# Rows of x turned and scaled in one product with a diagonal, and the modulation's weights behind x: the start of a hybrid decoder layer

## The chip, the cores and the metric

The kernel runs on one core of a Trainium2 chip, as one launch. The metric is device time in microseconds (us) of that core. Engines are named as the profile names them: PE is TensorE (matrix products; PEld is its weight load), DVE VectorE, ACT ScalarE, POOL GpSimd, SP SyncE. SPq and ACTq are the sequencers of SP and ACT as issuers of transfers.

## The reference, cut

One layer of a decoder trunk, batch 1, 512 tokens, width 2048, all float32. What matters here is its first lines:

```python
mod = silu(c) @ w_ada + b_ada                  # 1 x 6144
shift, scale, gate = split(mod, 3)
u = rms_norm(x, norm_w) * (1.0 + scale) + shift  # 512 x 2048
proj = u @ w_in                                # 512 x 23552
# ... three token mixers (attention, retention, dilated windows), each with its
# gate and projection, a gated sum m of the three, and
x = x + gate * (m @ w_out);  out = rms_norm(x, final_norm_w)
```

where `rms_norm(x, w) = x * rsqrt(mean(x*x) + 1e-6) * w`.

## The kernel before, in words

**Products.** A float32 product is done as three products of split operands. `h` is the value cast to PE's faster float32 form (`fp32r`), `l` the value minus `h`; then `uh*wh + ul*wh + uh*wl` go into one accumulator. So each weight tile needs a cast on ACT (`wh`) and a subtraction on DVE (`wl`, called the low part here), and each column block of u a `uh` on ACT and a `ul` on DVE. PE then runs three products of 512 columns for each block.

**The start.** u must stand with its 2048 channels on the partitions: 16 blocks k of 128 channels by 512 tokens, `xT[:, k, :]` before the modulation. x comes as 4 token tiles of 128x2048 (`xt[0..3]`, 1 MB each). For each tile ACT squares it and sums (`ss`), takes the root (`rstd`), DVE takes the reciprocal and multiplies the tile by it (`x_scale`); PE turns its 16 blocks with an identity (`x_tr`, 64 turns in all), and ACT copies each k from PSUM to `xT`. The small vectors (c, norm_w, b_ada and two more) come as 82 rows of `smalls` in five transfers and are turned on PE in one step to `cols`.

**The modulation.** The scale half of `mod` is worked out on DVE, not on PE: `mod_sum(m, part)` takes one 1 MB piece `wa` of w_ada and adds its rows, each times one entry of silu(c), into an accumulator `acc`; `mod_cols(m)` sums `acc` over the partitions with products against a column of ones (`pj<-ones,acc`), and two short DVE steps make `s1 = norm_w * (1 + scale)` of the group. `MODS` lists the groups: (half, first column, width). A group of 128 columns is one piece and 16 DVE steps of 128 columns, and gives `s1` for one k; a group of 256 is two pieces and 16 steps of 256 columns, for two k. Then `scaled(k)` makes `uh[k]` and `ul[k]` of `xT` and `s1`.

**Two passes over k.** The loop over `steps` has phase 0 (`uh`, `ul` without the shift; 16 steps of 21 products, 7 column blocks of w_in, on 7 accumulators) and phase 1 (with the shift, 16 such steps). Between the two, `spill` copies the seven accumulators to `raw` (two buffers) on ACT and DVE in turn, each copy followed by a transfer `graw` to memory on ACT's queue, and two more column blocks are done alone with four weight tiles of 128x1024 (`mids`, called the middle stage here; each tile needs its `wh` on ACT and its `wl` on DVE). During phase 0 DVE also does the sums of later groups (`mod_step`); the shift half (`sh`) is needed at the first step of phase 1. After that come the bulk of the projections, the mixers and the output, some 2370 us that this change leaves alone.

**What sets the order.** Each engine runs its instructions in a fixed order. At the places here a scheduler sets it when the kernel is built, by its own costs and by what is ready; `tc.issue_after(i)` holds a group of instructions behind instruction i, and `pin` (active where `pinned[0]` is true) keeps an engine's instructions in the order in which the code is written. Every recorded operation bears line 86 (`pin`) or its neighbour, so groups are told apart by the names of their tiles. SP issues all loads of x, `wa` and `wr` in one queue, in the order of the code; `wa` has 4 buffers, `wb` 3.

Of the kernel before, what the change touches and what calls it, by code (L numbers as in the profile page):

```python
# [65 lines left out]
def hybrid_kernel(ctx, tc, x, c, w_in, w_pa, w_pb, w_pc, w_out, w_ada, b_ada, norm_w, lam,  # L66
# [36 lines left out]
    def at():  # L103
        return psum.tile([P, 512], F32, tag="at", name="at", bufs=6)
# [120 lines left out]
    sync.dma_start(out=smalls[0:16, :], in_=c.rearrange("o (j p) -> (o j) p", p=P))  # L225
    sync.dma_start(out=smalls[16:32, :], in_=norm_w.rearrange("o (j p) -> (o j) p", p=P))
    sync.dma_start(out=smalls[32:80, :], in_=b_ada.rearrange("o (j p) -> (o j) p", p=P))
    sync.dma_start(out=smalls[80:81, :], in_=da_w)
    sync.dma_start(out=smalls[81:82, :], in_=ret_w)
# [11 lines left out]
    def mod_load():  # L241
        if not to_load:
            return
        i = len(parts) - len(to_load)
        m, part = to_load.pop(0)
        half, c0, cw = MODS[m]
        nk = 2048 // cw
        if i < 6 or (i - 6) % 7 >= 3:
            wa = sp.tile([P, nk, cw], F32, tag="wa", name="wa", bufs=4)
        else:  # L250
            wa = wb[0].tile([P, nk, cw], F32, tag="wb", name="wb", bufs=3)
        sync.dma_start(out=wa, in_=w_ada[0, part * nk * P:(part + 1) * nk * P, half * D + c0:half * D + c0 + cw]
                          .rearrange("(j p) c -> p j c", p=P))
        wa_tiles[m, part] = wa
# [101 lines left out]
    tps = [at() for _ in range(6)]  # L356
    for i in range(3):
        act.activation(out=xTf[:, i * D:(i + 1) * D], in_=xt[i], func=AF.Square, accum_out=ss[:, i:i + 1])
        if i == 0:
            act.activation(out=sgc, in_=c_col, func=AF.Sigmoid)  # L360
            dve.tensor_scalar(out=eps0, in0=sgc[:, 0:1], scalar1=0.0, scalar2=EPS, op0=ALU.mult, op1=ALU.add)
            dve.tensor_mul(sc, c_col, sgc)
            dve.tensor_scalar_mul(daw, cols[:, 80:81], 1.0 - LAM_INIT)
        x_scale(i)
        if i == 1:
            m, part = to_sum.pop(0)
            mod_sum(m, part)
        for k in range(6):
            x_tr(tps[k], i, k)
    for q in range(2):  # L370
        act.activation(out=xTf[:, 3 * D + q * 1024:3 * D + (q + 1) * 1024], in_=xt[3][:, q * 1024:(q + 1) * 1024],
                       func=AF.Square, accum_out=ss[:, 3 + q:4 + q])
    dve.tensor_add(ss[:, 3:4], ss[:, 3:4], ss[:, 4:5])
    x_scale(3)
    mod_cols(0)
# [6 lines left out]
    for k in range(KC):  # L382
        tp = tps[k] if k < 6 else at()
        for i in range(3 if k < 6 else 0, NT):
            x_tr(tp, i, k)
        act.copy(xT[:, k, :], tp)
        if k == 0:
            scaled(0)
            split_first(0)
            m, part = to_sum.pop(0)  # L390
            mod_sum(m, part)
            mod_cols(m)
        if k == 4:
            split_first(1)
# [14 lines left out]
    for i, (phase, k) in enumerate(steps):  # L409
# [1362 lines left out]
```

## Time and profile before

| what | value |
|---|---|
| median of 3 runs | 2574.26 us (2572.38 to 2576.52) |
| the profiled execution: its time, its span | 2571.79 us, 2570.0 us |
| mean granted clock of PE in it | 0.995 of full speed |
| PE busy | 2516.9 us, 98% |
| DVE busy | 1907.0 us, 74% |
| ACT busy | 1134.4 us, 44% |
| first main product of PE (`uh` by `wh`) | at 30.83 us |

The profile is one execution; its times run from the start of its span, and the 1.79 us between span and time lie around it. A busy share is an average over stages with different limits: what bounds one stage is read from that stage alone.

### The profile page before, as it was taken

The page shows a single profiled execution, that of the slowest core. Times are in us where ns is not written, and L with a number is a line of the kernel's source. Part 1 is how long each engine was busy: PE and PEld are TensorE (multiplying, and loading weights), DVE is VectorE, ACT ScalarE, POOL GpSimd, SP SyncE. Part 2 cuts the span into 40 slices and gives each one's busy share as a digit, 9 for nine tenths or more (in the row PEclk, how much of TensorE's full clock was granted, in tenths as well). Part 3 has the DMA queues.
Part 4 walks back from the last instruction along what each step waited for, and adds up shares of the span by engine and source line. Part 5 has one row for each costly group of instructions (what it writes and reads, how often), then busy time and mean ns, then how long its engine had stood idle before and what let it go on. Part 6 is the DMA issues. An engine that isn't in the chain of part 4 may idle for free. (4 is left out here: it accounts for less than half of the span.)

```text
span 2570.0 us, 36726 instructions
## 1 busy us (share of the span) xinstructions
PE 2516.9 (98%) x14539; PEld 2224.0 (87%) x14539; DVE 1907.0 (74%) x2716; ACT 1134.4 (44%) x1476; POOL 179.9 (7%) x293
## 2 busy tenths in 40 slices
PE   7999999999999999999999999999999999999998
PEld 6787777999999999999887888888888888778888
DVE  7885888778887788877886777347887657786554
ACT  5233433443444333333336666346666436652223
POOL 0000000000000000000000001200000220003100
PEclk9999999999999999999999999999999999999999
DMA  9886765666666666666556555654333673439533
GB/s 346 294 293 233 253 213 213 218 209 212 234 233 228 220 209 231 236 223 231 208 183 198 153 160 146 198 162 118 109 113 107 191 222 98 118 113 297 190 133 113
DMA packets 363953, 504.83 MB, mean 196 GB/s; under 512 B 18850, under 2 KB 237748, under 8 KB 363396
## 3 DMA queue, kind: packets, MB, share of 16 engines
q1 hardware_dynamic: 329732, 401.89, 47.8%
q0 software_dynamic: 27136, 92.13, 10.4%
q10 hardware_dynamic: 6912, 8.46, 0.9%
q8 instruction: 114, 1.87, 0.3%
q14 instruction: 59, 0.48, 0.1%
HBM read 450.37 MB, written 52.04 MB: 195 GB/s over the span
## 5 line engine op out<-in xcount | busy, mean ns | idle before, releaser
L86 ACT CAST xh<-xr 128x2048 fp32r<-128x2048 f32 x196 | 374.3, 1910 | 589.7 <-PE at L86 478.8
L86 DVE TENSOR_TENSOR xl<-xr,xh 128x2048 fp32r<-128x2048 f32 x196 | 448.9, 2290 | 184.9 <-ACT xh L86 183.5
L86 DVE TENSOR_TENSOR wl<-wr,wh 128x1024 fp32r<-128x1024 f32 (+2 forms) x275 | 275.4, 1018 | 186.2 <-ACT wh L86 181.4
L86 PE MATMUL pj<-uh,wl 128*128 128x512 f32 x944 | 368.6, 390 | 3.6 <-DVE wl L86 3.6
L86 PE MATMUL pj<-uh,wh 128*128 128x512 f32 x944 | 371.8, 394 | 0.0
L86 ACT CAST wh<-wr 128x1024 fp32r<-128x1024 f32 (+2 forms) x275 | 239.3, 889 | 294.8 <-PE at L86 137.9
L86 PE MATMUL pj<-ul,wh 128*128 128x512 f32 x944 | 368.5, 390 | 0.0
L86 DVE TENSOR_TENSOR xr<-xr 128x512 f32<-128x512 f32 x448 | 309.3, 690 | 13.8 <-DMA xr<-in_w_in_dram 2.3
L86 PE MATMUL at<-fh,xl 128*128 128x256 f32 x864 | 244.9, 283 | 0.7 <-DVE xl L86 0.7
L86 PE MATMUL at<-fh,xh 128*128 128x256 f32 x864 | 244.5, 283 | 0.0
L86 PE MATMUL at<-fl,xh 128*128 128x256 f32 x864 | 244.5, 283 | 0.0
L86 PEld LDWEIGHTS pj<-uh,wl 128*128 128x128 f32 x944 | 177.7, 188 | 41.7 <-DVE wl L86 4.0
L86 PEld LDWEIGHTS pj<-ul,wh 128*128 128x128 f32 x944 | 177.9, 188 | 35.4
L86 PEld LDWEIGHTS pj<-uh,wh 128*128 128x128 f32 x944 | 177.7, 188 | 35.3
L86 PEld LDWEIGHTS at<-fh,xl 128*128 128x128 f32 x864 | 165.8, 192 | 0.9 <-DVE xl L86 0.9
L86 PEld LDWEIGHTS at<-fh,xh 128*128 128x128 f32 x864 | 165.8, 192 | 0.0
L86 PEld LDWEIGHTS at<-fl,xh 128*128 128x128 f32 x864 | 165.8, 192 | 0.0
L86 PE MATMUL at<-uh,xh 128*128 128x256 f32 x576 | 163.0, 283 | 0.0
L86 PE MATMUL at<-ul,xh 128*128 128x256 f32 x576 | 163.0, 283 | 0.0
L86 PE MATMUL at<-uh,xl 128*128 128x256 f32 x576 | 163.0, 283 | 0.0
L86 PE MATMUL at<-yh,wh 128*128 128x512 f32 x288 | 113.1, 393 | 2.2 <-ACT wh L86 2.2
L86 PE MATMUL at<-yh,wl 128*128 128x512 f32 x288 | 112.8, 391 | 0.1
(387 smaller groups left out, 5595.5 us busy)
## 6 DMA issues: line engine op xcount, KB each, us to landing
xr<-in_w_in_dram SPq DMA_DIRECT2D x224, 512.0 KB, 4.5
xr<-in_w_in_dram SPq DMA_DIRECT2D x84, 1024.0 KB, 4.9
wr<-in_w_in_dram SPq DMA_DIRECT2D x116, 512.0 KB, 4.2
wa<-in_w_ada_dram SPq DMA_DIRECT2D x20, 1024.0 KB, 8.3
wr<-in_w_out_dram SPq DMA_DIRECT2D x32, 512.0 KB, 3.9
wr<-in_w_in_dram SPq DMA_DIRECT2D x32, 448.0 KB, 7.6
wb<-in_w_ada_dram SPq DMA_DIRECT2D x12, 1024.0 KB
bw<-in_w_in_dram SPq DMA_DIRECT2D x24, 384.0 KB, 5.5
```

Of the source, the lines that this page charges most:

```text
L86: return lambda *a, **k: pin(f(*a, **k))
```

## The change

It touches the start up to the first step of phase 0, and one condition in the loop.

1. The five transfers of `smalls` are issued by ACT, ahead of everything else there; SP's queue begins with x, in eight halves of 512 KB, all of them ahead of the first `wa`. Before, two tiles of x, the first `wa`, and then the other two.
2. The tiles of x are not scaled. For each tile ACT squares two halves (into the end of `xT`, which is free then), DVE adds the two sums, ACT takes the root, and DVE the reciprocal; then DVE makes `diag[i] = identity * rstd`, 128x128, and PE multiplies each block of x with it: `x_block.T @ diag` is turned and scaled at once. It is a true float32 product in place of a turn; there are 64, as there were turns.
3. Tiles 0 and 1 go first, as a pair: their 24 products for the first 12 blocks k, and DVE copies these to `xT` in six steps of two blocks by 256 tokens (a seventh a little later); tiles 2 and 3 follow. The other nine copies are ACT's.
4. `MODS` begins with four groups of 128 columns (two before).
5. The whole start is pinned to the order of the code, to the low part of the first weight tile; what of the sums comes after is held behind that low part.

```diff
-    sync.dma_start(out=smalls[0:16, :], in_=c.rearrange("o (j p) -> (o j) p", p=P))
...
+    pinned[0] = True
+    act.dma_start(out=smalls[0:16, :], in_=c.rearrange("o (j p) -> (o j) p", p=P))
...
-    for i in range(2):
-        sync.dma_start(out=xt[i], in_=x[0, i * P:(i + 1) * P, :])
-    MODS = [(1, 0, 128), (1, 128, 128)] + [(1, c0, 256) for c0 in range(256, D, 256)] \
+    for i in range(NT):
+        for q in range(2):
+            qs = slice(q * 1024, (q + 1) * 1024)
+            sync.dma_start(out=xt[i][:, qs], in_=x[0, i * P:(i + 1) * P, qs])
+    MODS = [(1, c0, 128) for c0 in range(0, 512, 128)] + [(1, c0, 256) for c0 in range(512, D, 256)] \
...
-    sync.dma_start(out=xt[2], in_=x[0, 2 * P:3 * P, :])
-    for q in range(2):
-        sync.dma_start(out=xt[3][:, q * 1024:(q + 1) * 1024], in_=x[0, 3 * P:4 * P, q * 1024:(q + 1) * 1024])
...
+    act.activation(out=sgc, in_=c_col, func=AF.Sigmoid)
+    dve.tensor_scalar(out=eps0, in0=sgc[:, 0:1], scalar1=0.0, scalar2=EPS, op0=ALU.mult, op1=ALU.add)
+    act.activation(out=warm, in_=eps0, func=AF.Sqrt)
+    dve.tensor_mul(sc, c_col, sgc)
...
+    def x_squares(i):
+        for q in range(2):
+            act.activation(out=junk, in_=xt[i][:, q * 1024:(q + 1) * 1024], func=AF.Square,
+                           accum_out=ss[:, 2 * i + q:2 * i + q + 1])
+        dve.tensor_add(ss[:, 2 * i:2 * i + 1], ss[:, 2 * i:2 * i + 1], ss[:, 2 * i + 1:2 * i + 2])
+        act.activation(out=rstd[:, i:i + 1], in_=ss[:, 2 * i:2 * i + 1], func=AF.Sqrt, scale=1.0 / D, bias=eps)
+    def x_norm(i):
         dve.reciprocal(rstd[:, i:i + 1], rstd[:, i:i + 1])
-        for q in range(2):
-            qs = slice(q * 1024, (q + 1) * 1024)
-            dve.tensor_scalar_mul(xt[i][:, qs], xt[i][:, qs], rstd[:, i:i + 1])
-    def x_tr(tp, i, k):
-        pe.transpose(tp[:, i * P:(i + 1) * P], xt[i][:, k * P:(k + 1) * P], ident)
...
+        dve.tensor_scalar_mul(diag[i], ident, rstd[:, i:i + 1])
+    def x_turn(tps, i, ns):
...
+                pe.matmul(tps[n][:, o * P:(o + 1) * P], lhsT=xt[i][:, (2 * n + k) * P:(2 * n + k + 1) * P],
+                          rhs=diag[i], start=True, stop=True)
+    def x_put(tps, pair, ns, copy):
+        for n in ns:
+            copy(xT[:, 2 * n:2 * n + 2, pair * 256:pair * 256 + 256], tps.pop(n).rearrange("p (k t) -> p k t", k=2))
+    x_squares(0)
+    x_norm(0)
+    x_squares(1)
+    x_norm(1)
+    x_turn(tps, 0, range(6))
+    x_turn(tps, 1, range(6))
+    x_put(tps, 0, range(6), dve.tensor_copy)
+    for i in range(2):
+        x_turn(tps, i, (6,))
+    x_squares(2)
+    x_norm(2)
+    x_put(tps, 0, (6,), dve.tensor_copy)
+    x_turn(tps, 2, range(6))
+    x_squares(3)
+    x_norm(3)
...
+    mod_sum(m, part)
+    for n in range(6):
+        x_turn(tps, 3, (n,))
+    x_put(tps, 1, range(5), act.copy)
+    x_turn(tps, 2, (6, 7))
+    x_turn(tps, 3, (6, 7))
+    mod_cols(0)
...
+    halves[0] = act.copy(firsts[0][1], firsts[0][0]).ins
+    act.activation(out=uh[0], in_=xT[:, 0, :], func=AF.Copy, scale=s1[:, 0:1])
...
+    low_part = dve.tensor_sub(l, r, h.bitcast(F32)).ins
+    pinned[0] = False
+    m, part = to_sum.pop(0)
+    with tc.issue_after(low_part):
+        mod_sum(m, part)
+    mod_cols(m)
+    split_first(1)
...
-        if phase == 0 and k > 0:
+        if phase == 0:
             with tc.issue_after(low_part):
-                mod_step()
+                mod_step(2 if i == 0 else 1)
         else:
-            mod_step(2 if i == 0 else 1)
+            mod_step()
```

What stands on DVE at three places, before and after. **First place: the norms of the token tiles.** Before, from the column step of the first group (`s1`) to the sum of the second group; `x2` and `x3` are token tiles being scaled, `wl_167` is the first weight tile's low part, `acc_271` the second group's accumulator.

```order
TENSOR_TENSOR s1_99<-pj_260,cols_97 128x1
SCALAR_TENSOR_TENSOR s1_99<-s1_99,cols_97 128x1
RECIPROCAL rstd_191<-rstd_191 128x1
TENSOR_SCALAR x2_156<-x2_156,rstd_191 128x1024 x2
TENSOR_TENSOR ss_190<-ss_190 128x1
TENSOR_TENSOR wl_167<-wr_165,wh_166 128x896
RECIPROCAL rstd_191<-rstd_191 128x1
TENSOR_SCALAR x3_157<-x3_157,rstd_191 128x1024 x2
TENSOR_SCALAR acc_271<-wa_169,sc_98 128x128 x2
```

After, from the last copies of the first pair of tiles to the sum of the first group (`acc_290`).

```order
COPY xT_201<-at_230 128x2x256
COPY xT_201<-at_233 128x2x256
TENSOR_TENSOR ss_199<-ss_199 128x1
RECIPROCAL rstd_200<-rstd_200 128x1
TENSOR_SCALAR diag2_204<-ident_88,rstd_200 128x128
COPY xT_201<-at_254 128x2x256
TENSOR_TENSOR ss_199<-ss_199 128x1
RECIPROCAL rstd_200<-rstd_200 128x1
TENSOR_SCALAR diag3_205<-ident_88,rstd_200 128x128
TENSOR_SCALAR acc_290<-wa_166,sc_98 128x128 x2
SCALAR_TENSOR_TENSOR acc_290<-wa_166,sc_98,acc_290 128x128 x14
TENSOR_TENSOR s1_99<-pj_334,cols_97 128x1
```

The adding of tile 2's two sums (the first `ss` row) has moved behind the six copies of the first pair, and the first group's sum, which stood ahead of tiles 2 and 3 before, behind the diagonal of tile 3.

**Second place: from the first `ul` to the second.** Before (`acc_271` second group, `wl_173` the second step's low part, `acc_401` third group of 256 columns):

```order
SCALAR_TENSOR_TENSOR ul0_122<-xT_192,s1_99,uh0_106 128x512
SCALAR_TENSOR_TENSOR acc_271<-wa_169,sc_98,acc_271 128x128 x10
TENSOR_TENSOR wl_173<-wr_171,wh_172 128x896
TENSOR_TENSOR s1_99<-pj_288,cols_97 128x1
TENSOR_SCALAR acc_401<-wa_175,sc_98 128x256
SCALAR_TENSOR_TENSOR s1_99<-s1_99,cols_97 128x1
TENSOR_SCALAR acc_401<-wa_175,sc_98 128x256
SCALAR_TENSOR_TENSOR acc_401<-wa_175,sc_98,acc_401 128x256 x6
SCALAR_TENSOR_TENSOR acc_401<-wa_177,sc_98,acc_401 128x256 x8
SCALAR_TENSOR_TENSOR ul1_123<-xT_192,s1_99,uh1_107 128x512
```

After (`wl_171` and `wl_177` the low parts of the first two steps; `acc_352`, `acc_412`, `acc_431` the second to fourth group, all of 128 columns):

```order
TENSOR_TENSOR wl_171<-wr_169,wh_170 128x896
TENSOR_SCALAR acc_352<-wa_173,sc_98 128x128 x2
SCALAR_TENSOR_TENSOR acc_352<-wa_173,sc_98,acc_352 128x128 x14
TENSOR_TENSOR wl_177<-wr_175,wh_176 128x896
TENSOR_TENSOR s1_99<-pj_369,cols_97 128x1
TENSOR_SCALAR acc_412<-wa_179,sc_98 128x128
SCALAR_TENSOR_TENSOR s1_99<-s1_99,cols_97 128x1
TENSOR_SCALAR acc_412<-wa_179,sc_98 128x128
SCALAR_TENSOR_TENSOR acc_412<-wa_179,sc_98,acc_412 128x128 x14
TENSOR_SCALAR acc_431<-wa_181,sc_98 128x128 x2
SCALAR_TENSOR_TENSOR acc_431<-wa_181,sc_98,acc_431 128x128 x14
SCALAR_TENSOR_TENSOR ul1_123<-xT_201,s1_99,uh1_107 128x512
```

Ahead of these twelve stands `ul0`. The first low part and the whole sum of the second group now stand between the two `ul`, and two sums of 128 columns in place of one of 256.

**Third place: the middle stage.** Before (`wl_983` and `wl_1018` are the low parts of the first and second of its four weight tiles, `raw_...` the copies of phase 0's accumulators, `acc_974` and `acc_1141` sums of the shift half):

```order
TENSOR_TENSOR wl_983<-wr_981,wh_982 128x1024
SCALAR_TENSOR_TENSOR acc_974<-wa_897,sc_98,acc_974 128x512
COPY raw_1052<-at_370 128x512
SCALAR_TENSOR_TENSOR acc_974<-wa_897,sc_98,acc_974 128x512
SCALAR_TENSOR_TENSOR acc_1141<-wb_979,sc_98,acc_1141 128x512
SCALAR_TENSOR_TENSOR acc_974<-wa_936,sc_98,acc_974 128x512
SCALAR_TENSOR_TENSOR acc_1141<-wb_979,sc_98,acc_1141 128x512
SCALAR_TENSOR_TENSOR acc_974<-wa_936,sc_98,acc_974 128x512
COPY raw_1058<-at_372 128x512
SCALAR_TENSOR_TENSOR acc_974<-wa_936,sc_98,acc_974 128x512
TENSOR_TENSOR wl_1018<-wr_1016,wh_1017 128x1024
```

After (`wl_1049` is the second tile's low part now, `wl_1103` the third's; the first, `wl_1014`, stands four rows ahead):

```order
TENSOR_TENSOR wl_1049<-wr_1047,wh_1048 128x1024
SCALAR_TENSOR_TENSOR acc_1005<-wa_928,sc_98,acc_1005 128x512
SCALAR_TENSOR_TENSOR acc_1172<-wb_1010,sc_98,acc_1172 128x512
SCALAR_TENSOR_TENSOR acc_1005<-wa_928,sc_98,acc_1005 128x512
SCALAR_TENSOR_TENSOR acc_1172<-wb_1010,sc_98,acc_1172 128x512
SCALAR_TENSOR_TENSOR acc_1005<-wa_928,sc_98,acc_1005 128x512
COPY raw_1083<-at_381 128x512
SCALAR_TENSOR_TENSOR acc_1005<-wa_928,sc_98,acc_1005 128x512
TENSOR_TENSOR wl_1103<-wr_1101,wh_1102 128x1024
```

The second low part has moved ahead of both copies of `raw`; the third stands behind one copy.

## Rows read from the trace of the kernel before

**Rows 1.** The page: busy time, share of the span and instructions.

```profile
PE 2516.9 (98%) x14539; PEld 2224.0 (87%) x14539; DVE 1907.0 (74%) x2716; ACT 1134.4 (44%) x1476; POOL 179.9 (7%) x293
```

**Rows 2.** Busy time by stretch, then PE's granted clock, DMA share, GB/s.

```profile
0.00:30.80 30.80, 14.23 (x72) 12.67 (x73) 20.01 (x65) 20.39 (x34) 0.20 (x4) 1.00 1.01 330
...
52.50:110.95 58.45, 58.45 (x279) 49.15 (x278) 55.06 (x117) 18.05 (x23) 0.00 (x0) 1.00 0.97 332
110.95:142.30 31.35, 27.73 (x119) 22.64 (x118) 24.40 (x35) 8.63 (x12) 0.00 (x0) 0.95 0.83 293
...
200.00:2570.00 2370.00, 2337.55 (x13707) 2074.40 (x13705) 1741.75 (x2383) 1061.19 (x1372) 179.72 (x289) 1.00 0.57 187
```

**Rows 3.** PE's waits from 30 to 210 us: total, times, longest.

```profile
PE pj L86 <- DVE wl L86: 3.6, 1, 3.6
PE at L86 <- DVE ul L86: 0.4, 1, 0.4
```

**Rows 4.** The timeline, 0 to 40 us: start, duration (groups: whole), idle before.

```profile
7.21 0.45 PE L86 MATMUL pj<-ident,smalls 128*128 128x128 f32 x1 [7.21 <-DMA smalls<-in_ret_norm_w_dram]
...
8.42 1.28 ACT L86 ACT_TABLE_LOAD   x1
...
13.27 1.54 PE L86 MATMUL at<-ident,x 128*128 128x128 f32 x6 [0.68 <-DVE x L86]
13.79 0.48 DVE L86 TENSOR_SCALAR acc<-wa,sc 128x128 f32<-128x128 f32 x2
...
17.05 1.04 ACT L86 ACTIVATE xT<-x 128x1024 f32<-128x1024 f32 x1
...
17.74 1.01 PE L86 MATMUL pj<-ones,acc 128*128 128x1 f32 x4 [2.93 <-DVE acc L86]
...
18.09 0.28 ACT L86 ACTIVATE rstd<-ss,eps 128x1 f32<-128x1 f32 x1
...
18.79 0.16 DVE L86 TENSOR_TENSOR s<-pj,cols 128x1 f32<-128x1 f32 x1 [0.84 <-PE pj L86]
...
22.65 6.22 PE L86 MATMUL at<-ident,x 128*128 128x128 f32 x29 [1.05 <-DVE x L86]
...
24.12 0.73 ACT L86 ACTIVATE uh<-xT,s 128x512 fp32r<-128x512 f32 x1
...
29.24 1.84 PE L86 MATMUL at<-ident,x 128*128 128x128 f32 x15
...
30.08 5.62 DVE L86 SCALAR_TENSOR_TENSOR acc<-wa,sc,acc 128x256 f32<-128x256 f32 x14
...
30.83 0.48 PE L86 MATMUL at<-uh,wh 128*128 128x512 f32 x1
...
35.62 0.75 DVE L86 SCALAR_TENSOR_TENSOR ul<-xT,s,uh 128x512 fp32r<-128x512 f32 x1
...
38.10 1.61 PE L86 MATMUL at<-ul,wh 128*128 128x512 f32 x6
```

**Rows 5.** The timeline of PE in the middle stage.

```profile
123.81 0.60 PE L86 MATMUL pj<-uh,wl 128*128 128x512 f32 x1 [3.62 <-DVE wl L86]
...
127.56 0.39 PE L86 MATMUL pj<-uh,wl 128*128 128x512 f32 x1
```

**Rows 6.** The timeline of DVE in the middle stage.

```profile
113.42 0.68 DVE L86 COPY raw<-at 128x512 f32<-128x512 f32 x1
114.02 0.74 DVE L86 SCALAR_TENSOR_TENSOR acc<-wa,sc,acc 128x512 f32<-128x512 f32 x1
...
121.27 0.69 DVE L86 COPY raw<-at 128x512 f32<-128x512 f32 x1 [3.86 <-DMA graw<-raw]
...
134.61 1.09 DVE L86 TENSOR_TENSOR wl<-wr,wh 128x896 fp32r<-128x896 f32 x1 [2.80 <-ACT wh L86]
...
139.64 0.15 DVE L86 TENSOR_TENSOR sh<-pj,cols 128x4 f32<-128x4 f32 x1
```

**Rows 7.** Transfers issued from 100 to 135 us: count, size, median us to landing.

```profile
graw<-raw ACTq DMA_DIRECT2D x8, 256.0 KB, 6.1
```

More of the change, by code (lines that the diff above doesn't have):

```diff
@@ L251, in mod_load @@
             wa = wb[0].tile([P, nk, cw], F32, tag="wb", name="wb", bufs=3)
-        sync.dma_start(out=wa, in_=w_ada[0, part * nk * P:(part + 1) * nk * P, half * D + c0:half * D + c0 + cw]
-                          .rearrange("(j p) c -> p j c", p=P))
+        for j0, j1 in ((0, nk // 2), (nk // 2, nk)) if i == 0 else ((0, nk),):
+            r0 = part * nk * P
+            sync.dma_start(out=wa[:, j0:j1, :],
+                           in_=w_ada[0, r0 + j0 * P:r0 + j1 * P, half * D + c0:half * D + c0 + cw]
+                           .rearrange("(j p) c -> p j c", p=P))
         wa_tiles[m, part] = wa
@@ L292, in hybrid_kernel @@
     sgc = sp.tile([P, KC], F32, tag="sgc", name="sgc")
-    ss = sp.tile([P, NT + 1], F32, tag="ss", name="ss")
+    act.activation(out=sgc, in_=c_col, func=AF.Sigmoid)
+    dve.tensor_scalar(out=eps0, in0=sgc[:, 0:1], scalar1=0.0, scalar2=EPS, op0=ALU.mult, op1=ALU.add)
+    act.activation(out=warm, in_=eps0, func=AF.Sqrt)
+    dve.tensor_mul(sc, c_col, sgc)
+    dve.tensor_scalar_mul(daw, cols[:, 80:81], 1.0 - LAM_INIT)
+    ss = sp.tile([P, 2 * NT], F32, tag="ss", name="ss")
     rstd = sp.tile([P, NT], F32, tag="rstd", name="rstd")
     xT = xp.tile([P, KC, S], F32, tag="xT", name="xT")
-    xTf = xT.rearrange("p k t -> p (k t)")
+    junk = xT[:, KC - 2:KC, :].rearrange("p k t -> p (k t)")
+    diag = [sp.tile([P, P], F32, tag=f"diag{i}", name=f"diag{i}") for i in range(NT)]
     def mod_sum(m, part):
@@ L356, in hybrid_kernel @@
[L356 to L375, printed above, removed]
+    def x_squares(i):
[4 more added lines that the diff above has]
+        act.activation(out=rstd[:, i:i + 1], in_=ss[:, 2 * i:2 * i + 1], func=AF.Sqrt, scale=1.0 / D, bias=eps)
@@ new lines, in x_norm @@
+    def x_norm(i):
+        dve.reciprocal(rstd[:, i:i + 1], rstd[:, i:i + 1])
+        dve.tensor_scalar_mul(diag[i], ident, rstd[:, i:i + 1])
+    def x_turn(tps, i, ns):
+        for n in ns:
+            if n not in tps:
+                tps[n] = at()
+            for k in range(2):
+                o = 2 * k + i % 2
+                pe.matmul(tps[n][:, o * P:(o + 1) * P], lhsT=xt[i][:, (2 * n + k) * P:(2 * n + k + 1) * P],
+                          rhs=diag[i], start=True, stop=True)
+    def x_put(tps, pair, ns, copy):
+        for n in ns:
+            copy(xT[:, 2 * n:2 * n + 2, pair * 256:pair * 256 + 256], tps.pop(n).rearrange("p (k t) -> p k t", k=2))
@@ L377, in scaled @@
+    tps = {}
+    x_squares(0)
[13 more added lines that the diff above has]
+    x_norm(3)
     def scaled(k):
@@ L380, in scaled @@
                                         in1=uh[k].bitcast(F32), op0=ALU.mult, op1=ALU.subtract).ins
[L382 to L394, printed above, removed]
+    m, part = to_sum.pop(0)
[6 more added lines that the diff above has]
+    mod_cols(0)
+    last = {}
+    for i in range(2):
+        x_turn(last, i, (7,))
+    halves[0] = act.copy(firsts[0][1], firsts[0][0]).ins
+    act.activation(out=uh[0], in_=xT[:, 0, :], func=AF.Copy, scale=s1[:, 0:1])
+    x_put(tps, 1, (5, 6, 7), act.copy)
+    x_put(last, 0, (7,), act.copy)
+    dve.scalar_tensor_tensor(out=ul[0], in0=xT[:, 0, :], scalar=s1[:, 0:1], in1=uh[0].bitcast(F32),
+                             op0=ALU.mult, op1=ALU.subtract)
+    r, h, l = firsts[0]
+    low_part = dve.tensor_sub(l, r, h.bitcast(F32)).ins
+    pinned[0] = False
+    m, part = to_sum.pop(0)
+    with tc.issue_after(low_part):
+        mod_sum(m, part)
+    mod_cols(m)
+    split_first(1)
     x_es.close()
```

11 lines of the change are left out of this document (4 added, 7 removed).

## The prediction

> **What bounds the kernel now.** Read the busy shares first: PE is busy 98% of the span [rows 1]. That alone says only that a change elsewhere must reach PE to count. The windows by stage say where PE is not full: 14.2 of the first 30.8 us, nothing lost from 52.5 to 110.95, 27.7 of 31.35 in the middle stage, and 32.5 us spread over the 2370 behind 200 us [rows 2]. So before 200 us PE is the limit from its first main product on, and its start time is passed on to the end. Then PE's waits, 30 to 210 us: one of 3.6 us for a low part `wl`, one of 0.4 us for a `ul` [rows 3]. The first is what the middle stage can give back; the start can only be moved. DVE is busy 55.1 of 58.45 us in the stage between [rows 2], so a delay of DVE that reaches PE early is not made up there either: PE needs every microsecond, and what it starts late it ends late.
>
> **The start, step by step.** Before, the first main product runs at 30.83 and the second step's `ul` products at 38.10 [rows 4]; I compare with the latter, since PE doesn't wait again (but for 0.4 us) till the middle stage.
>
> *To the first product with a diagonal.* `smalls` are turned at 7.21; I leave that, since five issues on ACT replace five on SP. The table load begins by 8.42 and takes 1.28 [rows 4], and now stands ahead of the squares, where it stood behind the first before. Squares of a half take 1.04, a root 0.28 [rows 4]. With a short warming root, tile 0 has its squares at 12.1; sum (0.2), root (0.3), reciprocal (0.2) and diagonal (0.3; two such 128x128 steps take 0.48 [rows 4]) follow: 13.2. Tile 1 takes 2.3 of squares more and the same tail: 15.9.
>
> *The price of a product.* The trace has no float32 product of 128 columns. A turn takes about 0.22 in the group at 13.27 (1.54 for six) and 0.11 in that at 29.24 (1.84 for fifteen), tails taken off [rows 4]: the two levels of PE's clock, 1.2 and 2.4 GHz, though the clock column prints 1.00 there [rows 2]. The products with ones are true float32 ones, and the first group's two of them leave four records [rows 4]: two where a turn leaves one. So I take twice a turn, 0.45 at the lower level and 0.24 at the higher. Lower end: every product at the higher level's price from the first. Upper end: 0.45 throughout. The Trainium skill, page "TensorE: Matmul & The Clock Gate", Terms, says that transpose mode is four times faster for FP32; by it a product would cost four turns, 0.45 at the higher level as well. No row shows it, and it is the second rival below.
>
> *When the clock rises.* After the 3.62 us wait in the middle stage PE runs nine products in 3.75 us that take 0.23 each later, and is then at its old rate [rows 5]; the granted clock of that stretch is 0.95 in the mean [rows 2]. I put eight products here at the lower level likewise, to 16.8, and the rest at the higher: the first pair's 24 end at 20.7.
>
> *The copies, and who stands behind them.* A DVE copy of a 128x512 bank takes 0.60 to the next instruction [rows 6]. The first can begin when tile 1's first two products are done, 18.6; six end at 22.2. Behind them on DVE stands the adding of tile 2's sums; behind that on ACT the root of tile 2 and, in ACT's pinned order, the squares of tile 3. So tile 3, whose data are long there, is squared from 22.8 to 25.1, and its diagonal is done at 26.1. Only then comes the first group's sum, 4.0 us (13.79 to 17.74 [rows 4]): 30.1. Its column products and `s1` take 1.05 to the first short step [rows 4] and 0.5 more with PE's queue of turns ahead: 32.0. `uh` takes 0.73 [rows 4]: first main product at 32.8, **2.0 later** than 30.83.
>
> *From there to the second `ul`.* DVE must do `ul` (0.66), the low part (1.0), the second group's sum (4.0), the second low part (1.0), the short steps (0.2), two sums (8.2) and `ul` (0.7): 15.8 from 32.8, so PE gets it at **48.7, 10.6 later** than 38.10. Before, four of the second group's steps stood ahead of `ul`, the first low part too, and the third group was one of 256 columns, 5.62 us for fourteen steps [rows 4] against 8.2 for two of 128. PE has then run 28 products and waits some 4.6 us. Ends: higher level from the first product, copies done at 20.1 and column products 0.8 shorter, +7.7; 0.45 throughout, PE alone has 60 products (27 us) ahead of the first column products, so main product at 43 and +20.8.
>
> What is removed is in this chain already: DVE's eight scalings (its own four diagonals and seven copies replace them) and seven of ACT's sixteen copies. Loads don't bind: at 330 to 332 GB/s [rows 2] x and the first `wa` (5.2 MB) are in by about 18, and each further `wa` with its share of `wr` some 4.5 later (22, 27, 31), needed at 26, 34.5, 39.7 and 43.8. If they came in after that, the sums would move with them.
>
> `smalls` on a queue of its own might land sooner. The nearest row is the spill on ACT's queue, 256 KB in 6.1 us beside SP's loads [rows 7], no quicker way. The Trainium skill, "DMA: Bandwidth & Descriptors", Queues, rings and completion order, says that the engines change between queues packet by packet; by it `smalls` would not wait for x and the chain could begin 1 to 2 us sooner, which would make the sum about 1.5 less.
>
> **The clock after the new wait.** A wait of 4.6 us is longer than that of 3.62 after which nine products took 3.75 instead of 2.05 [rows 5]: 1.7 lost. Against it the 0.4 us wait for `ul` [rows 3] is covered by it. **+1.2**; ends 0 and +1.7.
>
> **The middle stage.** Before, the second weight tile's low part stands on DVE behind a copy of `raw` that waits 3.86 us for the transfer of an earlier one [rows 6]; PE waits 3.62 for it and runs nine products at the lower level. Now that low part stands ahead of both copies. The wait and 1.7 of slow products go: **-5.4**. The third low part now stands behind one copy, which finds a buffer free.
>
> **The second pass.** What is late next is the shift. From DVE's first copy of the stage to the short step that makes `sh`, 113.42 to 139.64, it idles 3.86 and 2.80 [rows 6], and PE then finds its operand just in time. Asked 5.4 earlier, DVE has 6.7 of idle time to give, but copies of `raw` still stand in its queue and each waits for a landing of 6.1 [rows 7] with some 3 us of work between: about 3.3 stays, and the shift misses PE by about 2.1, the next steps by a little more. **+2.5**; ends 0 (all waits gone) and +5.4 (gain all given back).
>
> **Sum.** +10.6 +1.2 -5.4 +2.5 = +8.9 on the profiled execution's 2571.8, so 2580.7. The runs' median, 2574.3, is 2.5 above it: **2583**.
>
> **Rivals.**
> *The start is cheap and nothing is given back*: products at the higher level's price, no slow stretch after the wait, the shift in time: 7.7 - 5.4 = +2.3, 2576.6. For it: DVE's 6.7 us of idle time. Against: PE did run at the lower level for much of the start. Within 0.2%, which is 5 us and about what a measurement here can tell from no change.
> *Products are dear* (0.45 throughout): 20.8 + 1.2 - 5.4 + 2.5 = +19.1, 2593.4. For it: the page's rule. Against: the two records at 0.25 and less for ones.
> *Another wait takes the place of the one removed*, at the third low part: no -5.4, and no give-back: +11.8, 2586.
> *Faster*: the 32.5 us that PE loses behind 200 us [rows 2] shrink, because PE comes later to engines that run ahead of it. Place: the stages behind 200 us. Price: up to 32.5, so 2551 if all of it goes. It decides from 14.0 us on (8.9 + 5.1). Against: instructions there keep their order, and an engine that waits for PE's buffers doesn't get ahead.
> *The change doesn't do what it says*, the start not moved: the listed order leaves no room for it, and it isn't counted.
>
> **How the numbers follow.** Forecast (some 2578 to 2588) 0.53, cheap start 0.17, dear products 0.14, wait replaced 0.07, faster 0.09. Cases between forecast and cheap start fall on either side of 5 us, so 0.03 moves to the same: faster 0.09, same 0.20, slower 0.71. The range leaves out the faster case and the very dear products: 2573 to 2593.
>
> **What the profile after would show.** First product with a diagonal at 13.2, 0.45 then 0.24 apart; copies on DVE 18.6 to 22.2; tile 3's squares at 22.8; first main product at 32.8; PE waiting some 4.6 us for `ul` and running at 48.7; no wait for `wl` in the middle stage; a wait of 1 to 3 us at the start of phase 1. Wrong would make it: products below 0.2 or at 0.45 and more, a clock that stays low to 30, sums overlapped otherwise on DVE, or `smalls` landing far from 7.2.

## The result and the profile after

| | median of the runs | beside the kernel before, same chip | ratio, 95% interval |
|---|---|---|---|
| changed, first measured | 2585.34 us (4 runs, 2582.32 to 2587.09) | 2574.0 (4 runs) | 1.0043 (1.0032 to 1.0055) |
| changed, once more beside the experiments | 2582.72 us (5 runs, 2581.95 to 2588.58) | 2574.68 (27 runs) | 1.0035 (1.0021 to 1.0049) |

The changed kernel is slower, by 11.3 and by 8.0 us between medians. The profiled execution took 2586.33 us, with a span of 2584.6, 14.6 longer than the one before. The forecast was 2583 us, in a range of 2573 to 2593.

PE's waits from 30 to 220 us in the profile after (total, times, longest), in place of [rows 3]:

```profile
PE at L86 <- ACT uh L86: 4.6, 3, 3.4
PE at L86 <- DVE ul L86: 4.3, 1, 4.3
PE pj L86 <- DVE acc L86: 2.1, 2, 1.1
```

The wait for `wl` is gone, as forecast; a wait for `ul` of 4.3 us and one for `uh` of 3.4 us have come. Where they stand is seen in the timeline of the start (start, duration, idle before), in place of [rows 4]:

```profile
7.63 0.45 PE L86 MATMUL pj<-ident,smalls 128*128 128x128 f32 x1 [7.63 <-DMA x<-in_x_dram]
...
13.43 8.98 PE L86 MATMUL at<-diag,x 128*128 128x128 f32 x56 [5.36 <-DVE diag L86]
...
19.33 3.68 DVE L86 COPY xT<-at 128x512 f32<-128x512 f32 x6 [3.21 <-PE at L86]
...
23.31 1.04 ACT L86 ACTIVATE xT<-x 128x1024 f32<-128x1024 f32 x1
...
24.02 7.43 PE L86 MATMUL at<-diag,x 128*128 128x128 f32 x64 [1.61 <-issue]
...
26.97 3.76 DVE L86 SCALAR_TENSOR_TENSOR acc<-wa,sc,acc 128x128 f32<-128x128 f32 x14
...
33.05 0.97 PE L86 MATMUL at<-uh,wh 128*128 128x512 f32 x3 [0.26 <-ACT uh L86]
...
40.30 3.76 DVE L86 SCALAR_TENSOR_TENSOR acc<-wa,sc,acc 128x128 f32<-128x128 f32 x14
...
44.37 3.76 DVE L86 SCALAR_TENSOR_TENSOR acc<-wa,sc,acc 128x128 f32<-128x128 f32 x14
48.05 0.75 DVE L86 SCALAR_TENSOR_TENSOR ul<-xT,s,uh 128x512 fp32r<-128x512 f32 x1
...
48.85 2.93 PE L86 MATMUL at<-ul,wh 128*128 128x512 f32 x6 [4.35 <-DVE ul L86]
```

It can be read as the chain of the prediction: products from 13.4, copies from 19.3, tile 3's squares only at 23.3 behind them, the first group's sum from 26.6, the first main product at 33.05 (30.83 before [rows 4]), two sums of 128 columns, and the second step's `ul` products at 48.85 (38.10 before [rows 4]). The last row's six products take 2.93 us where they took 1.61 [rows 4]: PE is at the lower level after the wait.

DVE in the middle stage after, in place of [rows 6]:

```profile
121.97 1.23 DVE L86 TENSOR_TENSOR wl<-wr,wh 128x1024 fp32r<-128x1024 f32 x1 [0.38 <-issue]
...
131.57 0.69 DVE L86 COPY raw<-at 128x512 f32<-128x512 f32 x1 [1.34 <-DMA graw<-raw]
...
140.13 0.69 DVE L86 COPY raw<-at 128x512 f32<-128x512 f32 x1 [5.22 <-DMA graw<-raw]
...
151.25 0.15 DVE L86 TENSOR_TENSOR sh<-pj,cols 128x4 f32<-128x4 f32 x1
...
158.68 0.55 DVE L86 TENSOR_SCALAR uf<-xT,s,sh 128x512 f32<-128x512 f32 x1 [2.78 <-DMA ud<-uf]
```

The second low part, at 121.97, is long there when PE wants it. But DVE now waits 1.34 and 5.22 us for landings of `graw`, 6.56 in all, where it idled 3.86 and 2.80 before [rows 6], and `sh` is made at 151.25. The last row shows a wait of a second kind: in the second pass each step's u with the shift (`uf`, two buffers) is sent to memory by a transfer `ud`, and DVE waits 2.78 us for one of these to land. PE's side of it, and then busy time in three stretches (PE, PEld, DVE, ACT, POOL; the last three figures are PE's granted clock, DMA share and GB/s):

```profile
152.96 2.50 PE L86 MATMUL at<-uh,wh 128*128 128x512 f32 x5 [3.44 <-ACT uh L86]
```

```profile
48.80:54.00 5.20, 5.15 (x15) 4.09 (x16) 5.20 (x13) 2.52 (x3) 0.00 (x0) 0.62 1.08 360
121.00:143.00 22.00, 22.00 (x98) 18.21 (x97) 15.05 (x21) 5.56 (x8) 0.00 (x0) 1.00 0.86 282
152.90:158.00 5.10, 5.04 (x12) 3.98 (x13) 3.00 (x5) 1.85 (x4) 0.00 (x0) 0.50 1.05 396
```

PE is full and at 1.00 through the middle stage, and behind each of the two new waits it runs at the lower level, in the mean 0.62 and 0.50 of full speed over these windows.

### The profile page after: what moved, and what is told of

Its sections match the earlier page's. It is cut to its first block, busy times and chain, and to the rows that moved or that the text cites. A ratio compares the mean times of both kernels' runs of the same rounds, so it can differ in the third digit from the quotient of the medians.

```text
span 2584.6 us, 36882 instructions
## 1 busy us (share of the span) xinstructions
PE 2525.0 (98%) x14603; PEld 2231.8 (86%) x14603; DVE 1909.7 (74%) x2740; ACT 1132.5 (44%) x1476; POOL 178.9 (7%) x293
```

## The experiments

Theories: **A**, DVE's chain and its amount of work set the start (A1: the place of two sums ahead of the second `ul`; A2: how much is still to be done when PE's first main product starts). **B**, the price of the float32 products does. **E**, the loads behind x do. For the stage behind: **C**, the landings of `raw` transfers hold DVE; **D**, DVE's sums of the shift half do.

The table gives, of each profile, the start of the first main product and of the second step's `ul` products, and how late the same product, counted in PE's order, is against the profile before, at four places (there at 60.21, 138.14, 144.12 and 180.16 us: first pass, end of the middle stage, first and eighth step of the second pass). The last two columns are the median of the runs, and its ratio to the kernel before on the same chip.

| kernel | first main | second `ul` | late at 60 | 138 | 144 | 180 | median | ratio, interval |
|---|---|---|---|---|---|---|---|---|
| before | 30.83 | 38.10 | 0 | 0 | 0 | 0 | 2574.0 | 1 |
| changed | 33.05 | 48.85 | 12.34 | 7.04 | 12.41 | 13.18 | 2585.34 | 1.0043 (1.0032 to 1.0055) |
| changed, again | 33.28 | 49.07 | 12.72 | 7.20 | 11.43 | 12.32 | 2582.72 | 1.0035 (1.0021 to 1.0049) |
| turns for products | 30.20 | 45.99 | 9.68 | 4.16 | 8.86 | 9.65 | 2582.74 | 1.0043 (1.0029 to 1.0057) |
| two sums late | 33.79 | 43.39 | 12.05 | 7.76 | 10.43 | 12.60 | 2584.55 | 1.0042 (1.0029 to 1.0055) |
| two narrow groups | 32.96 | 47.35 | 10.84 | 5.32 | 7.37 | 9.40 | 2584.73 | 1.0044 (1.0030 to 1.0058) |
| third raw buffer | 33.77 | 49.57 | 13.18 | 7.66 | 8.08 | 11.57 | 2579.61 | 1.0027 (1.0017 to 1.0037) |
| first sum early | 32.32 | 44.69 | 8.80 | 3.28 | 4.99 | 10.61 | 2580.38 | 1.0024 (1.0015 to 1.0033) |
| before, third raw buffer | 30.48 | 37.76 | -0.33 | -4.10 | -3.91 | 1.95 | 2575.41 | 1.0001 (0.9993 to 1.0010) |
| first sum early, two narrow groups, third raw buffer | 32.51 | 43.46 | 7.14 | 6.70 | 6.70 | 7.21 | 2575.19 | 1.0004 (0.9996 to 1.0013) |
| first piece early | 32.27 | 48.07 | 12.66 | 7.15 | 10.58 | 11.82 | 2584.52 | 1.0036 (1.0023 to 1.0048) |
| norm 2 ahead of copies | 31.48 | 47.27 | 11.73 | 10.55 | 12.70 | 14.92 | 2584.18 | 1.0036 (1.0023 to 1.0048) |
| before, five buffers | 31.00 | 38.28 | 0.21 | -1.12 | 2.90 | 3.06 | 2574.18 | 1.0000 (0.9991 to 1.0009) |
| first sum early, two narrow groups, five buffers | 32.12 | 42.51 | 5.25 | -0.27 | 1.21 | 0.97 | 2575.18 | 1.0002 (0.9993 to 1.0011) |

A profile is one execution. One kernel's executions lie some 4 to 9 us apart, so what a step moves is read from the profile at its place, and what it is worth in all from the medians.

**Turns for products.** This kernel leaves the scaling by the norm out.

```diff
-        dve.tensor_scalar_mul(diag[i], ident, rstd[:, i:i + 1])
+        dve.tensor_scalar(out=diag[i], in0=ident, scalar1=rstd[:, i:i + 1], scalar2=0.0, op0=ALU.mult, op1=ALU.is_gt)
...
-                pe.matmul(tps[n][:, o * P:(o + 1) * P], lhsT=xt[i][:, (2 * n + k) * P:(2 * n + k + 1) * P],
-                          rhs=diag[i], start=True, stop=True)
+                pe.transpose(tps[n][:, o * P:(o + 1) * P], xt[i][:, (2 * n + k) * P:(2 * n + k + 1) * P], diag[i])
```

> The changed kernel with turns in place of the 64 float32 products: the diagonal is made of zeros and ones at the same place, with the same waits, and PE turns with it (the norm of x is left out of the output). Theory A, DVE's chain sets the start: only the first copies can begin earlier, by about 2.2 us (19.33 to about 17), and all behind them; second step's ul products at 46 to 46.7 instead of 48.85, total 2 to 3 us shorter. Theory B, the price of the products sets the start: 64 records of 0.12 to 0.16 us go, 8 us of PE's time; first main product at 29 or before instead of 33.05, second ul at 43 or before, total 5 us shorter or more.

The timeline: copies and the last turns of the start, start and duration.

```profile
17.09 3.68 DVE L86 COPY xT<-at 128x512 f32<-128x512 f32 x6 [0.79 <-PE at L86]
...
24.50 2.48 PE L86 MATMUL at<-diag,x 128*128 128x128 f32 x20 [1.20 <-DVE diag L86]
```

The copies begin at 17.09, 2.24 earlier, and the second `ul` comes 2.86 earlier, at 45.99: theory A, to the number. PE now has gaps between its turns and waits as long for `ul`, so its own time was hidden but for those 2 to 3 us. Twenty turns take 2.48 us and 64 records of products 7.43: 0.12 a record in both, and a product leaves two records. In the total the gain doesn't show (1.0043 again).

**Two sums late.**

```diff
+            if k == 1:
+                with tc.issue_after(low_part):
+                    mod_step()
...
-        if phase == 0:
+        if phase == 0 and k > 0:
             with tc.issue_after(low_part):
-                mod_step(2 if i == 0 else 1)
+                mod_step(2 if i == 2 else 1)
+        elif phase == 0:
+            pass
```

> The changed kernel with the sums of the third and fourth group held behind the second ul (and the next group's behind the third ul). Theory A1, it is the place of these sums ahead of the second ul that costs: ul products at about 42 instead of 48.85, the wait of 4.35 us and the slow products behind it gone, total 6 to 7 us shorter. Theory A2, it is the amount of DVE work that is still to be done when the first main product starts: the second ul comes at 42, but PE waits for ul or uh of the steps 3 to 6 instead, by 60 to 80 us it is late by 10 or more again, total 0 to 2 us shorter. Theory B, price of the products: as A1 for the second ul, since PE's start is not touched.

PE's waits from 38 to 75 us, in its timeline:

```profile
39.39 0.38 PE L86 MATMUL pj<-ones,acc 128*128 128x1 f32 x2 [1.10 <-DVE acc L86]
41.67 1.65 PE L86 MATMUL at<-uh,wh 128*128 128x512 f32 x6 [0.87 <-ACT uh L86]
48.39 1.66 PE L86 MATMUL at<-uh,wh 128*128 128x512 f32 x6 [1.33 <-ACT uh L86]
50.79 0.65 PE L86 MATMUL pj<-ones,acc 128*128 128x1 f32 x4 [0.52 <-DVE acc L86]
51.72 1.66 PE L86 MATMUL at<-ul,wh 128*128 128x512 f32 x6 [0.28 <-DVE ul L86]
58.53 1.23 PE L86 MATMUL pj<-ones,acc 128*128 128x1 f32 x8 [1.76 <-DVE acc L86]
```

The long wait is cut to pieces and handed on, and at 60 us PE is late by 12.05 instead of 12.34. A1 falls, A2 stands: not where the sums stand costs, but how much DVE has still to do.

**Two narrow groups.**

```diff
-    MODS = [(1, c0, 128) for c0 in range(0, 512, 128)] + [(1, c0, 256) for c0 in range(512, D, 256)] \
+    MODS = [(1, 0, 128), (1, 128, 128)] + [(1, c0, 256) for c0 in range(256, D, 256)] \
```

> The changed kernel with the old list of groups (two of 128 columns, then 256). Theory A2, amount of DVE work: third group is 6.1 us in place of 8.2 for two, second ul products at 46.8 instead of 48.85, the wait shrinks to about 2.3, total 2 to 3 us shorter. Theory B or a start bound by loads: no change beyond 0.5 us.

The third group's steps are fourteen of 256 columns again (5.62 us in this timeline), the second `ul` starts at 45.88 on DVE instead of 48.05, 2.2 less as A2 has it; PE gets to it at 47.35, since the column products come in between, and stays 1.5 ahead of the changed kernel at 60 us. The total doesn't tell it from the changed kernel.

**Third raw buffer.**

```diff
-    diag = [sp.tile([P, P], F32, tag=f"diag{i}", name=f"diag{i}") for i in range(NT)]
+    diag = [xq.tile([P, P], F32, tag=f"diag{i}", name=f"diag{i}") for i in range(NT)]
...
-        raw = wbp.tile([P, S], F32, tag="raw", name="raw", bufs=2)
+        raw = wbp.tile([P, S], F32, tag="raw", name="raw", bufs=3)
```

> The changed kernel with three buffers for raw in place of two (the diagonals lie in the pool of x to make room). Theory C, the give-back behind the middle stage comes from copies of raw that wait for the landing of an earlier transfer on DVE and ACT: these waits shrink below 1.5 us each, the shift is in time, the wait of 3.44 us at the start of the second pass and its slow products go, total 5 to 6 us shorter (2580). Rival D, DVE's and ACT's own work up to the shift is too long: the wait at the second pass stays above 2.5 us, total 0 to 1 us shorter.

DVE in the middle stage, then PE at the fifth step of the second pass:

```profile
132.83 0.69 DVE L86 COPY raw<-at 128x512 f32<-128x512 f32 x1 [2.43 <-DMA graw<-raw]
134.76 0.68 DVE L86 COPY raw<-at 128x512 f32<-128x512 f32 x1
...
148.31 0.16 DVE L86 TENSOR_TENSOR sh<-pj,cols 128x4 f32<-128x4 f32 x1
```

```profile
172.31 2.18 PE L86 MATMUL at<-uh,wh 128*128 128x512 f32 x6 [1.79 <-ACT uh L86]
```

One wait of 2.43 is left of 6.56, `sh` is made 2.9 us earlier though DVE started 0.8 later, PE has no wait at the first step, and it is late by 8.08 instead of 12.41 at 144 us. C holds at this place. Then the second group of the shift, which the fifth step is the first to need, is late: a wait of 1.79 there, slow products again, 11.57 at 180 us. By the ratios the total is 2 to 4 us shorter (1.0027 after 1.0043 and 1.0035), where 5 to 6 were expected; the intervals overlap.

**First sum early.** The loads in the old order (below), and in the start:

```diff
     x_norm(1)
+    m, part = to_sum.pop(0)
+    mod_sum(m, part)
     x_turn(tps, 0, range(6))
     x_turn(tps, 1, range(6))
-    x_put(tps, 0, range(6), dve.tensor_copy)
...
     x_squares(2)
     x_norm(2)
-    x_put(tps, 0, (6,), dve.tensor_copy)
+    x_put(tps, 0, range(6), dve.tensor_copy)
+    mod_cols(0)
...
+    x_put(tps, 1, (0,), act.copy)
+    scaled(0)
```

> The changed kernel with the first group's piece loaded between tiles 1 and 2 as before, its sum done on DVE in the idle time ahead of the first copies, tile 2's norm ahead of these copies, and uh and ul of the first step made as soon as their block of xT is there. Theory A2, DVE lost the work that it did ahead of PE's first main product: some 4 us of sum go into idle time, ul of the first step is done 4 to 5 us earlier than at 33.8, second ul products at 44 to 45 instead of 48.85, still with a wait, late by 7 to 8 at 60 us instead of 12.3; total 3 to 5 us shorter than the changed kernel. Theory B, products or loads set the start: first main product not earlier than 32.5 and the second ul later than 47.

```profile
16.55 3.76 DVE L86 SCALAR_TENSOR_TENSOR acc<-wa,sc,acc 128x128 f32<-128x128 f32 x14
...
28.88 0.75 DVE L86 SCALAR_TENSOR_TENSOR ul<-xT,s,uh 128x512 fp32r<-128x512 f32 x1 [2.88 <-ACT uh L86]
```

`ul` of the first step is done 4.15 us earlier than in the changed kernel (28.88 against 33.03), the second `ul` products run at 44.69, 4.2 earlier, and at 60 us PE is late by 8.80, where 7 to 8 were expected. At 144 us it is 4.99. Then the fifth step takes it back: a wait of 2.71 there (timeline, at 170.11), and 10.61 at 180. The total is 1.0024. Three things were moved together here; the load order alone and the norm of tile 2 alone, below, move the second `ul` by 0.8 and 1.6 us of these 4.2.

**First piece early**, the load order alone:

```diff
-    for i in range(NT):
+    def x_load(i):
         for q in range(2):
             qs = slice(q * 1024, (q + 1) * 1024)
             sync.dma_start(out=xt[i][:, qs], in_=x[0, i * P:(i + 1) * P, qs])
+
+    x_load(0)
+    x_load(1)
...
     mod_load()
+    x_load(2)
+    x_load(3)
     load_first(0)
```

> The changed kernel with the loads in the old order alone (first piece of the modulation's weights between tiles 1 and 2 of x, all else as changed). Theory A2, DVE's work and its place: the sum still stands behind tile 3's norm, so nothing moves by more than 0.5 us; second ul products at 48.5 to 49.5, total as the changed kernel within 1.5 us. Rival E, the loads behind x are what delays the start: second ul 2 us or more earlier.

The first main product is 0.8 to 1.0 earlier, the second `ul` too, more than the 0.5 expected of A2 and less than the 2 of E. At 60 us nothing is left of it (12.66). E falls at this size. The piece has to be summed early, not only to be there.

**Norm 2 ahead of copies.**

```diff
     x_turn(tps, 1, range(6))
+    x_squares(2)
+    x_norm(2)
     x_put(tps, 0, range(6), dve.tensor_copy)
...
-    x_squares(2)
-    x_norm(2)
     x_put(tps, 0, (6,), dve.tensor_copy)
```

> The changed kernel with the norm of tile 2 ahead of the six copies on DVE. Step of the prediction, the adding of tile 2's sums behind the copies holds tile 3 and the first group's sum: diagonal of tile 3 done at about 24 instead of 26.7, PE's gap of 1.6 us between the pairs closes, first main product at 31.5 (1.5 earlier), second ul at 47.3; then PE's products are the bound, so no more than that. If the copies did not hold it: no change.

31.48 and 47.27: the step of the prediction, to the number. The gap between the pairs is closed (120 records in one run from 13.72, 16.16 us). The rest of the run goes otherwise: DVE's two copies of `raw` wait 4.29 and 5.05 us for landings in this profile, PE waits 2.46 us for a low part at 145.25, and the gain is gone. It doesn't show in the total (1.0036).

**Before, third raw buffer** (the second edit of the third raw buffer above, alone, on the kernel before).

> The kernel before with three buffers for raw in place of two, nothing else. Theory C, landings of raw transfers set the middle stage and what follows: PE's wait of 3.62 us and the nine slow products behind it go in part or whole, 3.5 to 5.4 us earlier at 138 us, and with the copies no longer waiting most of it stays at the second pass; total 2 to 5 us shorter than before. Rival D, the shift's sums are the next limit whatever the copies do: the gain is given back by 165 us, total within 1 us of before.

```profile
121.29 0.50 PE L86 MATMUL pj<-uh,wl 128*128 128x512 f32 x1 [1.44 <-DVE wl L86]
161.57 2.93 PE L86 MATMUL at<-uh,wh 128*128 128x512 f32 x6 [3.06 <-ACT uh L86]
```

These are all of PE's waits from 115 to 185 us. The 3.62 us are down to 1.44, and PE is 4.10 early at 138 us; at the fifth step of the second pass it waits 3.06 for the second shift group and runs at the lower level, and is 1.95 late at 180. So what the middle stage can give, the next stage takes, and the total is 1.0001, as D has it. But the cause that D names isn't shown by it. On the way to the second group's `sh` DVE isn't out of time; it waits twice for landings of `ud`, 4.20 us in all (0.92 before):

```profile
143.64 0.55 DVE L86 TENSOR_SCALAR uf<-xT,s,sh 128x512 f32<-128x512 f32 x1 [2.69 <-DMA ud<-uf]
146.36 0.55 DVE L86 TENSOR_SCALAR uf<-xT,s,sh 128x512 f32<-128x512 f32 x1 [1.51 <-DMA ud<-uf]
```

**Before, five buffers**:

```diff
-        raw = wbp.tile([P, S], F32, tag="raw", name="raw", bufs=2)
+        raw = wbp.tile([P, S], F32, tag="raw", name="raw", bufs=5)
...
-            uf = wbp.tile([P, S], F32, tag="uf", name="uf", bufs=2)
+            uf = wbp.tile([P, S], F32, tag="raw", name="uf", bufs=5)
```

> The kernel before with five buffers shared by raw and uf in place of two and two. If only the landings hold DVE (theory C in full): PE's wait in the middle stage and the later ones for uf all go, 4 to 5 us earlier at 138 us and still at 180 us, total 3 to 5 us shorter than before. Rival D, DVE's sums of the shift half have to be done by then and there is no time left for them: what the middle stage gains is given back by 180 us, total within 1.5 us of before.

Now the waits for `graw` on DVE are down to 0.54 and those for `ud` are gone; PE still waits 2.62 us at the first step of the second pass, and the total is 1.0000. That wait isn't for a late sum, as D has it. DVE's order has changed with the buffers:

```profile
121.96 0.16 DVE L86 TENSOR_TENSOR sh<-pj,cols 128x4 f32<-128x4 f32 x1 [0.55 <-PE pj L86]
...
137.62 5.09 DVE L86 SCALAR_TENSOR_TENSOR acc<-wa,sc,acc 128x512 f32<-128x512 f32 x7
142.63 1.00 DVE L86 TENSOR_SCALAR uf<-xT,s,sh 128x512 f32<-128x512 f32 x2
...
160.14 1.09 DVE L86 TENSOR_TENSOR wl<-wr,wh 128x896 fp32r<-128x896 f32 x1 [3.67 <-PE pj L86]
```

The first `sh` is made at 121.96, 17.7 us earlier than before [rows 6], and the `uf` that PE needs stands behind seven steps of the next group's sums; later DVE idles 3.67 us for PE. So this run doesn't decide between C and D.

**The repairs together**, with three buffers and with five.

> The changed kernel with the first group's sum early, two groups of 128 columns as before, and three raw buffers: the three repairs together. If they add (A2 and C): second ul products at 42.5 to 43.5, late by 5 to 6 us at 60 us, by 0 to 1 at 138 us and by 1 to 2 at 165 us; total within 2.5 us of before. If one delay only makes room for another (rival): total 6 us or more above before, as near to the changed kernel as single repairs.

> The changed kernel with the first group's sum early, two groups of 128 columns and five shared buffers for raw and uf. Late by 5 to 7 us at 60 us as with three buffers; by 1 to 3 at 165 and 180 us with no wait above 1 us in the second pass; total from 2 us shorter to 3 us longer than before. If DVE's sums are the limit (D): a wait of 2 us or more for uh at the first or the fifth step of the second pass.

The second `ul` products run at 43.46 and 42.51. With three buffers the second low part stands behind a copy of `raw` again, which waits 4.95 us for a landing, and PE waits 3.18 for that low part, so that PE is late by 7.14 at 60 us and 6.70 at 138, where 5 to 6 and 0 to 1 were expected; the median is 2575.19 all the same, and the profiled execution, at 2579.07, was the slowest of the eleven. With five, these are all of DVE's waits from 110 to 165 us (total, times, longest):

```profile
DVE wl L86 <- ACT wh L86: 1.4, 2, 0.7
DVE raw L86 <- PE at L86: 0.2, 1, 0.2
```

None is for a landing, where the changed kernel has 9.3 us of them in the same stretch and the repairs with three buffers 7.4. PE is 0.27 early at 138 us and 0.97 late at 180, and its one wait in the second pass is 1.19 us. So in the profiles the give-back goes with the waits for landings, of `graw` and of `ud`: C, and at most the 1.19 for D. In the medians three and five buffers are the same. Both totals are those of the kernel before (1.0004 and 1.0002): the repairs undo the loss, and neither beats it. No version here beats the kernel before.

> The changed kernel once more, so that the next three are compared with it on one chip. Expected as first measured: 1.0043 of before, second ul products at 48 to 49.5, wait of 3 to 4 us at the start of the second pass.

That run is the second row of the table above: 1.0035, and 49.07 for the second `ul`. Its wait at the start of the second pass is 2.45 us, less than the 3 to 4 expected.

## Why the prediction was right, and which term was off

| step | forecast | measured in the profile after |
|---|---|---|
| first product with a diagonal | 13.2 | 13.43 |
| copies on DVE | 18.6 to 22.2 | 19.33 to 23.01 |
| squares of tile 3 | 22.8 | 23.31 |
| first main product | 32.8 | 33.05 |
| second `ul` products | 48.7, +10.6 | 48.85, +10.74 |
| slow products behind that wait | +1.2 | +1.6 (12.34 at 60 us) |
| middle stage | -5.4 | -5.3 (12.34 to 7.04) |
| second pass | +2.5, ends 0 and +5.4 | +6.1 (7.04 to 13.18); +5.1 in the second profile |
| sum | +8.9 | +13.2 at 180 us, +14.6 in span; medians +11.3 and +8.0 |

**The start** went as worked out, and two experiments give the reason: the norm of tile 2 put ahead of the copies, and turns for products, each moved the chain by what its step says. Theory A1, the place of the two sums ahead of the second `ul`, fell. What holds is A2. Before, DVE was busy 13.05 of the 14.90 us from 10.0 to 24.9 (third pair of the first row), with `ul` of the first step started at 24.89, 5.9 us ahead of PE's first main product [rows 4]. The second row is the kernel after, ahead of its first copy:

```profile
10.00:24.90 14.90, 7.89 (x33) 6.59 (x34) 13.05 (x39) 9.33 (x17) 0.00 (x0) 1.00 1.10 358
9.00:19.30 10.30, 5.87 (x30) 5.87 (x31) 1.22 (x6) 8.26 (x16) 0.00 (x0) 1.00 1.05 340
```

There DVE is busy 1.22 of 10.30 us, `ul` starts with the first main product, and 15.0 us of DVE work stand between the first `ul` and the second where 10.7 did (24.89 to 35.62). 5.9 of lead and 4.3 of work, less 1.7 by which the second `ul` was ready early (36.4 done, 38.1 used), make 8.5; with the first main product's 2.2 that is the 10.7 measured. Inside this chain two errors offset each other. PE's records stayed at the lower pace till between 18 and 20 us (windows in the last section), not till 16.8, so that the first copy came 0.7 late and the end of the first sum 0.6 (30.73, forecast 30.1); and the column products and `uh` behind it took 2.3 us, not 2.7. The prediction also counts four steps of the second group's sum ahead of the first `ul` of the kernel before; six of the sixteen stand there, which changes no term.

**The price of a product** was taken as two turns: 64 records in 7.43 us are 0.23 a product, against 0.24 forecast. The Trainium skill, page "TensorE: Matmul & The Clock Gate", Terms, calls transpose mode four times faster for FP32; the runs here show two, and the measurement decides. The dear rival and its 2593 fall.

**The term that was off** is the last one: "about 3.3 stays, and the shift misses PE by about 2.1". It was mis-sized. DVE's waits for landings were 6.56 us (5.34 in the second profile), not 3.3, so of the 6.7 us of idle time that I let DVE give, it gave nothing in the first profile: the copies of ACT and DVE take the two buffers in turn, and each pair waits for the landing of the one ahead. PE then came 3.44 us short and lost a second stretch to the lower level (0.50 from 152.9 to 158.0), which I hadn't priced at this place at all. The third raw buffer shows the first part: 8.08 instead of 12.41 at 144 us. What then still is late at the fifth step came behind waits of DVE for `ud` (2.81 us with the third raw buffer, 4.20 with it on the kernel before), which the prediction didn't have; with five buffers on the repaired kernel both kinds of wait and all but 1.19 us of PE's are gone. The measured +6.1 lies above my upper end of +5.4, the +5.1 of the second profile just below it.

**The totals.** The sum was 4 us short of the profile at 180 us and 2.3 and 0.3 us from the two medians (2583 against 2585.34 and 2582.72). That the medians are so much nearer is luck: the two profiled executions lie 14.5 us apart, 3.2 more than the medians of the first measurement, and this hides most of what the last term missed. Rival "cheap start" falls with its price of 7.7; "another wait in its place" did not come at the third low part, but a wait of the same size came one stage later; the faster case did not show, the stages behind 200 us changed by 1 us either way (13.18 at 180 to 14.28 near the end in one profile, 12.32 to 11.01 in the other).

**Open**: why single repairs that bring PE 1.5 to 2.7 us earlier at 60 us (turns, two narrow groups) don't show in the medians. With intervals of 0.13 to 0.14% either way, 3 to 4 us, they need not. Open, too, is why the kernel before doesn't get faster with three or five buffers, and how much of the give-back would be left to DVE's own sums if its order stayed the same.

## What to carry to other kernels

An engine that is not the bound can become it when its head start is taken away: look at what it does in the idle time ahead of the main loop, and at what the reordering puts there instead. Before counting an engine's idle time as slack, see what ends that idle time: DVE's 6.66 us in the middle stage were waits, and 6.56 were there again after the change. Where a scheduler sets the order, an edit at one place changes the order at another (the middle stage with five buffers here), so read each variant's waits over the whole stretch and not only at the edit.

## What the runs showed of the hardware

A float32 product of 128 columns cost two turns of the same size, 0.23 us at the higher level, as two records. Each of PE's waits of 4.35 and 3.44 us in the changed kernel, and of 2.71 and 3.06 in experiments, was followed by products at the lower level; the windows above give 0.62 and 0.50. In the experiment with turns the first main products, behind turns and a wait of 0.76 us, ran at 0.50 as well; those of the changed kernel, behind true products and a wait of 0.26, ran at 1.00 (33.0 to 36.0).

```profile
30.20:33.30 3.10, 3.10 (x7) 2.48 (x8) 3.10 (x9) 1.88 (x4) 0.00 (x0) 0.50 1.17 307
```

In the first 20 us the clock column prints 1.00 throughout, but the records of the products stand 0.21 us apart till 18.5 us and 0.11 from there on, as the counts in these windows of the profile after show (PE's busy time with its count first):

```profile
16.00:18.00 2.00, 2.00 (x11) 2.00 (x11) 0.12 (x1) 1.79 (x4) 0.00 (x0) 1.00 1.19 302
18.00:20.00 2.00, 2.00 (x17) 2.00 (x16) 0.67 (x2) 0.00 (x0) 0.00 (x0) 1.00 1.13 342
...
24.00:28.00 4.00, 3.98 (x35) 4.00 (x36) 2.46 (x10) 2.42 (x7) 0.00 (x0) 1.00 1.17 307
```

Eleven records in 2 us, then 17, then 35 in 4. The transfers of `smalls` gained nothing from a queue of their own: they were turned at 7.63, and at 7.21 when SP issued them [rows 4]. But they didn't wait for x. These are the two queues of the changed kernel in its first 8 us, SP's and ACT's (packets, MB, share of the engines):

```profile
q1 hardware_dynamic: 615, 1.80, 66.6%
q10 hardware_dynamic: 132, 0.04, 2.1%
```

All 132 packets of `smalls` had gone when less than half of x's 4.2 MB had. The Trainium skill, "DMA: Bandwidth & Descriptors", Queues, rings and completion order, says that the engines change between queues packet by packet, and the trace agrees with it. The gain of 1 to 2 us that the prediction drew from it did not come: the last of the five was issued at 3.35 us by ACT and at 3.41 by SP before, and x stood ahead of them in SP's queue with one tile alone.
